# Both layers' MLP in blocks of 512 features, the first layer's with four seven-product pairs

## The chip, the cores and the metric

The kernel runs on one core of one Trainium2 chip. The metric is the device time of one execution in microseconds; the kernel before takes 2318.97 us, the median of three timed runs.

## What is computed

A trunk of two layers works on 640 tokens (128 context tokens, then 512 latent tokens) of width 1024. Each layer has a token mixer and a squared-ReLU MLP; the change touches the MLP.

```python
    sh1, sc1, g1, sh2, sc2, g2 = jnp.split(mod, 6, axis=-1)
    ...
    h = rmsnorm(x, lp['norm2_g']) * (1.0 + sc2) + sh2
    f = jnp.square(jax.nn.relu(h @ lp['w_mlp_in'])) @ lp['w_mlp_out']
    return x + g2 * f, k, v
```

`w_mlp_in` is 1024 by 4096, `w_mlp_out` is 4096 by 1024. `mod` comes from the conditioning vector of each group of tokens, so a residual add has one gain for columns 0 to 127 and another for columns 128 to 639.

## The kernel before, in words

**Layout.** Channels lie on the 128 partitions, the 640 tokens along the free dimension. Every float32 matrix is multiplied as two parts, h (rounded) and l (what is left): `split` (L239) makes h with an ACT copy (L240) and l with a DVE subtraction (L241), and a product takes three matmuls (h by h, h by l, l by h). A matmul covers 320 tokens, half of them, so a tile of 128 output channels with eight chunks of 128 inputs takes 8 x 3 x 2 = 48 matmuls, and one with four chunks 24.

**Weights.** They come as slabs of 128 by 1024 (512 KB). `ORDER` lists the slabs of each layer: `("i", j)` is the j-th 128 features of `w_mlp_in`, `("f", b, m)` is channel tile m of `w_mlp_out` for the 1024 features of block b, and `("h", b, i)` holds channel tiles 2i and 2i+1 for the 512 features of block b. `advance` has SP load them up to three ahead into four `raw` buffers and splits them up to two ahead into three pairs of buffers `wh`/`wl`. ACT and DVE work in an order that a scheduler fixes when the program is built; each engine then goes through its list in order. PE and SP follow the order of the code. Two priorities move instructions up in the scheduler's list: `SPLIT_FIRST` for weight splits and `EVAC_FIRST` for what empties PSUM.

**First layer's MLP before.** 32 input tiles (48 matmuls each) in four blocks of 8, each followed by ReLU on ACT (L1310), a square on DVE (L1311) and a split; after each block but the last, eight output tiles of 48 matmuls, each added to x by `residual` (L554) in three pieces (128, 192 and 320 columns). The last block goes through `project`, which also starts the next norm. PSUM has two buffers `ps`, one `sc`, one `pt`, one `po`. Beside this, `mod_dots` computes the second layer's modulation on DVE: 48 steps, each a load of 512 KB and two sums of products over 1024 columns (L490); `tick` moves it on by one step after each of these tiles.

**Second layer's MLP before** (`fast_mlp`). Six plain input tiles, then 13 pairs. A pair makes two input tiles from seven products of 12 matmuls (`prod`, L653) instead of 2 x 48 matmuls: 84 in place of 96. The products use sums of the activations' quarters (`t1` to `t4`, made once for each of four chunks on DVE, L627 to L638, and split into 16 tiles `t`) and sums of the weights (`one`, `two`, `three` in `Feed.pair`, L327 to L335). The first product of a pair is p1 (in `pt`, its right side the activations themselves), the second p5 (in `po`, its right side t1). `plus` (L659) adds the products up, L713 is ReLU and square in one. Between the products stand output tiles of blocks of 512 features (24 matmuls each); four per pair, until the last four pairs have 4, 2, 2 and 0.

## Time and profile before

| | us |
|---|---|
| median of 3 timed runs (2317.82 to 2321.76) | 2318.97 |
| the profiled execution, its own time | 2326.15 |
| its span, first to last instruction | 2324.4 |
| PE busy | 2254.2 (97%) |
| DVE busy | 1655.0 (71%) |
| ACT busy | 856.4 (37%) |

The first layer's MLP lies between about 734 and 1190 us of the span, the second layer's between about 1875 and 2324 us. Busy shares are averages over stages; what a change in one stage is worth shows in that stage, by the matmuls that PE starts in it and by what its gaps wait for.

### The profile page before, as it was taken

What the parts mean: (1) busy time and instruction counts of PE and PEld (TensorE: products, weight loads), DVE (VectorE), ACT (ScalarE), POOL (GpSimd) and SP (SyncE); (2) the same over time, 40 slices, a digit from 0 to 9 for tenths busy, and PEclk for the clock granted to TensorE, in tenths of its full rate; (3) what the DMA queues carried; (4) which work ended last, traced back from release to release, by engine and by line L of the source; (5) the groups of instructions that cost most, each with busy time, mean ns of one, the idle gap of its engine ahead of it and who ended that gap; (6) DMA issues with size and microseconds to landing.
All of it is one profiled execution on the core that took longest, in us unless ns stands there. A gap on an engine that the chain in (4) does not pass through costs nothing.

```text
span 2324.4 us, 36290 instructions
## 1 busy us (share of the span) xinstructions
PE 2254.2 (97%) x15050; PEld 2182.7 (94%) x15050; DVE 1655.0 (71%) x2557; ACT 856.4 (37%) x1296; POOL 70.4 (3%) x188
## 2 busy tenths in 40 slices
PE   6999999999999999999999999999999999999997
PEld 5989899989999999999998898999999999999987
DVE  6676457678777776766477773687897788777776
ACT  5455342222335332222254553422224453232233
POOL 1100000000000000000011000000000000000001
PEclk9999999999999999999999999999999999999999
DMA  7421122333343444444354212222222432222223
GB/s 285 113 84 60 63 70 99 133 136 136 126 138 127 154 154 146 151 148 146 108 175 107 78 46 69 73 78 64 65 76 92 150 109 65 73 85 89 73 91 110
DMA packets 77253, 252.43 MB, mean 109 GB/s; under 512 B 11808, under 2 KB 12832, under 8 KB 76960
## 3 DMA queue, kind: packets, MB, share of 16 engines
q1 hardware_dynamic: 66592, 224.56, 29.9%
q0 software_dynamic: 9920, 24.89, 3.8%
q8 instruction: 118, 1.93, 0.3%
q10 hardware_dynamic: 576, 0.66, 0.1%
q14 instruction: 47, 0.39, 0.1%
HBM read 238.65 MB, written 10.75 MB: 107 GB/s over the span
## 4 chain that ended last, share of the span: by engine, by line
PE 66%; issue 24%; DVE 6%; ACT 2%; DMA 1%; POOL 0%; SPq 0%; DVEq 0%; ACTq 0%; POOLq 0%
PE ps L362 44%; PE ph L362 5%; PE pt L653 4%; DVE l L241 2%; PE sc L653 2%; PE pt L857 1%; PE sc L846 1%; PE po L865 1%; PE sc L362 1%; ACT h L240 1%; PE po L653 1%; PE sc L1031 1%; DMA st<-in_w_mod 1%; PE pt L447 1%; PE sc L414 1%
## 5 line engine op out<-in xcount | busy, mean ns | idle before, releaser
L362 PE MATMUL ps<-h,h 128*128 128x320 f32 x5296 | 1119.3, 310 | 12.8 <-ACT gx L1132 4.7
L362 PEld LDWEIGHTS ps<-h,h 128*128 128x128 f32 x5296 | 862.7, 188 | 31.9 <-ACT h L240 12.5
L362 PE MATMUL ps<-h,l 128*128 128x320 f32 x3408 | 835.7, 309 | 0.0
L240 ACT ACTIVATE h<-raw 128x1024 fp32r<-128x1024 f32 x337 | 357.2, 1060 | 976.7 <-PE ps L362 658.8
L362 PEld LDWEIGHTS ps<-h,l 128*128 128x128 f32 x3408 | 585.6, 188 | 0.0
L241 DVE TENSOR_TENSOR l<-raw,h 128x1024 fp32r<-128x1024 f32 x337 | 411.6, 1222 | 217.5 <-ACT h L240 217.1
L362 PE MATMUL ps<-l,h 128*128 128x320 f32 x1520 | 384.6, 308 | 0.0
L362 PEld LDWEIGHTS ps<-l,h 128*128 128x128 f32 x1520 | 263.9, 188 | 0.3
L973 DVE SCALAR_TENSOR_TENSOR cv<-cv,cw,cv 128x655 f32<-128x655 f32 x240 | 215.9, 899 | 6.1
L554 DVE SCALAR_TENSOR_TENSOR x<-ps,mod,x 128x128 f32<-128x128 f32 (+2 forms) x260 | 99.8, 434 | 117.9 <-PE ps L362 117.8
L362 PE MATMUL ph<-h,h 128*128 128x320 f32 x768 | 179.6, 318 | 0.0
L362 PEld LDWEIGHTS ph<-h,h 128*128 128x128 f32 x768 | 129.1, 188 | 7.2
L240 ACT ACTIVATE h<-tmp 128x640 fp32r<-128x640 f32 (+1 forms) x92 | 67.5, 737 | 138.7 <-DVE tmp L1311 79.9
L362 PE MATMUL ph<-h,l 128*128 128x320 f32 x384 | 118.5, 309 | 0.0
L362 PE MATMUL ps<-bo,h 128*128 128x320 f32 x512 | 96.5, 309 | 1.8 <-DVE mg L1144 1.8
L241 DVE TENSOR_TENSOR l<-pt,h 128x512 fp32r<-128x512 f32 x84 | 57.9, 689 | 41.5 <-ACT h L240 41.3
L362 PEld LDWEIGHTS ps<-bo,h 128*128 128x128 f32 x512 | 80.2, 188 | 5.1 <-DVE mg L1144 2.4
L241 DVE TENSOR_TENSOR l<-tmp,h 128x640 fp32r<-128x640 f32 x92 | 74.9, 816 | 8.3 <-ACT h L240 8.3
L240 ACT ACTIVATE h<-pt 128x512 fp32r<-128x512 f32 x84 | 50.3, 599 | 77.1 <-PE pt L857 70.8
L490 DVE SCALAR_TENSOR_TENSOR junk<-raw,sw 128x1024 f32<-128x1024 f32 x48 | 58.8, 1224 | 25.4 <-DMA raw<-in_w_modt 25.2
L653 PE MATMUL pt<-h,h 128*128 128x320 f32 x260 | 71.4, 309 | 2.6 <-DVE tmp L659 2.6
L362 PEld LDWEIGHTS ph<-h,l 128*128 128x128 f32 x384 | 72.1, 188 | 0.0
(300 smaller groups left out, 2573.9 us busy)
## 6 DMA issues: line engine op xcount, KB each, us to landing
raw<-in_slabs SPq DMA_DIRECT2D x324, 512.0 KB, 3.6
raw<-in_w_modt SPq DMA_DIRECT2D x48, 512.0 KB, 3.7
md<-in_w_mod SPq DMA_DIRECT2D x32, 512.0 KB, 4.4
q<-qd POOLq DMA_DIRECT2D x18, 256.0 KB, 3.1
st<-in_w_mod SPq DMA_DIRECT2D x8, 512.0 KB, 9.7
raw<-in_w_mod SPq DMA_DIRECT2D x8, 512.0 KB, 7.1
x<-in_x SPq DMA_DIRECT2D x8, 320.0 KB, 6.0
qd<-h POOLq DMA_DIRECT2D x8, 320.0 KB, 9.1
```

What stands on the lines that cost most here:

```text
L240: act.activation(h, src, AF.Copy)
L241: (eng or vec).tensor_tensor(lo, src, _f(h), ALU.subtract)
L362: pe.matmul(v[:, c0:c1] if half is None else v, w_[:, kk, :], x_[:, c0:c1], start=first and pi == 0, stop=last and pi == 2)
L414: pe.matmul(v[:, c0:c1], ones, src[:, c0:c1], start=True, stop=True)
L447: pe.matmul(t[32 * q:32 * q + 32], sv3[:, 2 * kp + i, :], rr[i][j], start=kp == 0, stop=kp == 3)
L490: vec.scalar_tensor_tensor(out, w, 0.5, s3[s], ALU.mult, ALU.mult, accum_out=dst[:, c, s:s + 1])
L554: vec.scalar_tensor_tensor(xc[:, c0:c1], v[:, c0 - b0:c1 - b0], gv[:, c, s:s + 1], xc[:, c0:c1], ALU.mult, ALU.add)
L653: pe.matmul(v, w_[:, k0 + k, :], x_, start=k == 0 and pi == 0, stop=k == 3 and pi == 2)
L846: pe.matmul(v[:, c0:c1], lq, kk[:, SEQ + c0:SEQ + c1], start=pi == 0, stop=pi == 1)
L857: pe.transpose(pt[:, qt * P:(qt + 1) * P], parts[hd, qt][:, j * P:(j + 1) * P], ident)
L865: pe.matmul(po, vt[:, 1 + j, hd // 4, :], halves[hd, j][pi], start=j == 0 and pi == 0, stop=j == 4 and pi == 1)
L973: vec.scalar_tensor_tensor(y, b[:, j:j + CO], cw[:, c * CONV_K + j:c * CONV_K + j + 1], y, ALU.mult, ALU.add)
```

## The change

- The first layer gets the second layer's form: blocks of 512 features. Its first 24 input tiles are plain (48 matmuls each); from the fifth on, each is followed by the two output tiles of one `"h"` slab (24 matmuls each) for the block before. The last 8 input tiles are four seven-product pairs with 4, 2, 2 and 0 output tiles. The last 1024 features go through `project` as before. The second layer keeps six plain tiles and 13 pairs.
- `mod_dots` now moves on by two or three steps per plain input tile, and ends before the pairs; its buffers are given back, and the pairs' buffers are opened in their place. The quarter sums (`sums`) stand behind that point in the first layer, and beside the fifth tile, as before, in the second. The first layer, which doesn't keep the normed activations whole, adds h and l up again.
- The first layer's squares go from DVE to ACT for plain tiles. Residual adds of plain output tiles take two pieces (128 and 512 columns) in both layers.
- The first layer's slabs are loaded up to the layer's end by `Feed`; `advance` starts again at the second layer's first slab.

```diff
-FAST = (1,)
+PLAIN = (24, 6)
...
-    if l in FAST:
-        r += [("i", j) for j in range(5)] + [("h", 0, 0), ("i", 5), ("h", 0, 1)]
-        for b, p, fs in PAIRS:
-            r += [("i", 4 * b + 2 * p + i) for i in range(2)] + [("h", *f) for f in fs]
-        return r + 2 * [("f", 3, m) for m in range(8)]
-    r += [("i", j) for j in range(8)]
-    for b in range(4):
-        if b < 3:
-            r += [("i", 8 * (b + 1) + j) for j in range(8)]
-        r += [("f", b, m) for m in range(8)] * (2 if b == 3 else 1)
-    return r
+    r += [("i", j) for j in range(4)]
+    for j in range(4, PLAIN[l]):
+        r += [("i", j), ("h", j // 4 - 1, j % 4)]
+    for b, p, fs in PAIRS[l]:
+        r += [("i", 4 * b + 2 * p + i) for i in range(2)] + [("h", *f) for f in fs]
+    return r + 2 * [("f", 3, m) for m in range(8)]
...
+        def out_plain(w, m, fb):
+            v = _run(mtile(w, fb, k0=4 * (m % 2)))
+            for c0, c1, s in SEGS:
+                with later(-EVAC_FIRST):
+                    vec.scalar_tensor_tensor(x[m][:, c0:c1], v[:, c0:c1], mod3(l, 5)[:, m, s:s + 1], x[m][:, c0:c1], ALU.mult, ALU.add)
+
+        def sums():
...
+            for k in range(4):
+                s = tmp(T)
+                t1, t2 = s[:, a0:a1], s[:, b0:b1]
+                (h1, l1), (h2, l2) = ((_f(z) for z in h[k + n]) for n in (0, 4))
+                if keep:
+                    y1, y2 = keep[k], keep[k + 4]
+                else:
+                    y1, y2 = tmp(TH), tmp(TH)
+                    for y, (hh, lo) in ((y1, (h1, l1)), (y2, (h2, l2))):
+                        vec.tensor_tensor(y, hh[:, b0:b1], lo[:, b0:b1], ALU.add)
+                vec.tensor_tensor(t1, y1, h1[:, a0:a1], ALU.subtract)
+                vec.tensor_tensor(t1, t1, l1[:, a0:a1], ALU.subtract)
+                vec.tensor_tensor(t2, y2, t1, ALU.subtract)
+                if not keep:
+                    vec.tensor_tensor(y2, y2, y1, ALU.subtract)
+                    tb.append((k, y2))
+                    rest(k, s, y2, tslot, tb)
+                ta.append(split(s, tslot, T))
...
+        def rest(k, s, t3, tslot, tb):
+            h2, l2 = (_f(z)[:, a0:a1] for z in h[k + 4])
+            u = tmp(T)
+            vec.tensor_tensor(u[:, b0:b1], h2, l2, ALU.add)
+            vec.tensor_tensor(u[:, b0:b1], u[:, b0:b1], s[:, b0:b1], ALU.subtract)
+            vec.tensor_copy(u[:, a0:a1], t3)
+            tb[-1] = split(u, tslot, T)
...
+        for j in range(4, PLAIN[l]):
+            b, i = divmod(j, 4)
+            v = relu2(_run(mtile(use("i", j), h)))
+            fs_.setdefault(b, []).append(v)
+            tick()
+            if keep and j == 4:
+                quarters = sums()
+            w = use("h", b - 1, i)
+            for m in (2 * i, 2 * i + 1):
+                out_plain(w, m, fs_[b - 1])
+                if m % 2 or j % 2:
+                    tick()
+        if not keep:
+            flush()
+            dots.close()
+            open_room()
+        fd = Feed(room[0], (l + 1) * NS)
...
+        feed.append(fd)
+        fd.pump()
+        ta, tb = quarters or sums()
...
-                vec.tensor_tensor(r, r, r, ALU.mult)
+                if l + 1 < DEPTH:
+                    act.activation(r, r, AF.Square)
+                else:
+                    vec.tensor_tensor(r, r, r, ALU.mult)
...
+            if l + 1 < DEPTH:
+                nxt["dma"] = nxt["split"] = (l + 1) * NS
+                nxt["cap"] = ENDS[l + 1]
```

How the built programs' orders differ is shown at three places; in the rows a number behind a name tells one buffer's use from another's.

**PE, first layer's MLP, behind its 24th input tile, before.** `ps_9870` is the last output tile of the second block, `ps_9933` the 25th input tile (`h_6629` the activations, `h_9803` its weights).

```order
L362 MATMUL ps_9870<-h_8371,h_9740 128x320 x2
L362 MATMUL ps_9870<-l_8372,h_9740 128x320 x2
L362 MATMUL ps_9870<-h_8371,l_9741 128x320 x2
L362 MATMUL ps_9933<-h_6629,h_9803 128x320 x2
L362 MATMUL ps_9933<-h_6630,h_9803 128x320 x2
L362 MATMUL ps_9933<-h_6629,l_9804 128x320 x2
```

**PE at the same place, now.** `pt_10378` is the first pair's p1, which follows the last plain output tile `ps_10222` directly; `po_10393` is its p5 (`h_10311` and `l_10312` are the first chunk of t1, `h_10332` and `l_10333` the second, `h_10353` and `l_10354` the third, `h_10273` the weights).

```order
L702 MATMUL pt_10378<-h_6635,h_10269 128x320
L702 MATMUL pt_10378<-h_6636,h_10269 128x320
L702 MATMUL pt_10378<-h_6635,l_10270 128x320
L702 MATMUL po_10393<-h_10311,h_10273 128x320
L702 MATMUL po_10393<-l_10312,h_10273 128x320
L702 MATMUL po_10393<-h_10311,l_10274 128x320
L702 MATMUL po_10393<-h_10332,h_10273 128x320
L702 MATMUL po_10393<-l_10333,h_10273 128x320
L702 MATMUL po_10393<-h_10332,l_10274 128x320
L702 MATMUL po_10393<-h_10353,h_10273 128x320
L702 MATMUL po_10393<-l_10354,h_10273 128x320
```

The plain 25th tile has given way to a pair, whose second product reads what the quarter sums make; p1 is 12 matmuls, and p5 follows it at once.

**DVE at the same place, before.** The last output tile of the second block is added to x, with steps of `mod_dots` (`junk`, L490) and weight splits around it.

```order
L554 SCALAR_TENSOR_TENSOR x_6588<-ps_9870,mod_78,x_6588 128x128
L554 SCALAR_TENSOR_TENSOR x_6588<-ps_9870,mod_78,x_6588 128x192
L554 SCALAR_TENSOR_TENSOR x_6588<-ps_9870,mod_78,x_6588 128x320
L490 SCALAR_TENSOR_TENSOR junk_10125,mod_79<-raw_10056,sw_7571 128x1024
L241 TENSOR_TENSOR l_9930<-raw_9864,h_9929 128x1024
```

**DVE at the same place, now.** The last plain output tile `ps_10222` is added to x; around it stand the quarter sums (L630 to L633, L635, L655 to L657), of which those of the first chunk end with `l_10308` and `l_10312`.

```order
L615 SCALAR_TENSOR_TENSOR x_6588<-ps_10222,mod_78,x_6588 128x128
L615 SCALAR_TENSOR_TENSOR x_6588<-ps_10222,mod_78,x_6588 128x512
L657 COPY tmp_10303<-tmp_10296 128x320
L631 TENSOR_TENSOR tmp_10315<-tmp_10316,h_6631 128x320
L238 TENSOR_TENSOR l_10287<-raw_10257,h_10286 128x1024
L330 TENSOR_TENSOR raw_10277<-raw_10265,raw_10277 128x512
L655 TENSOR_TENSOR tmp_10324<-h_6639,h_6640 128x320
L632 TENSOR_TENSOR tmp_10315<-tmp_10315,h_6632 128x320
L238 TENSOR_TENSOR l_10308<-tmp_10303,h_10307 128x640
L238 TENSOR_TENSOR l_10312<-tmp_10294,h_10311 128x640
L633 TENSOR_TENSOR tmp_10315<-tmp_10317,tmp_10315 128x320
L630 TENSOR_TENSOR tmp_10337<-h_6633,h_6634 128x320
```

From the first of these rows to the last quarter sum's split there are 38 rows: 2 on `ps_10222`, 22 of 320 columns, 4 copies of 320, 8 splits of 640 (two for each chunk), one of 1024 and one of 512.

**DVE, the first layer's last pair, now**, the third place, in the step to `project`, whose first tile is `ps_11193`. Before, three output tiles of 48 matmuls stood here.

```order
L708 TENSOR_TENSOR tmp_11120<-pt_11123,tmp_11118 128x320
L751 SCALAR_TENSOR_TENSOR tmp_11163<-tmp_11120 128x640
L238 TENSOR_TENSOR l_11160<-raw_11023,h_11159 128x1024
L708 TENSOR_TENSOR tmp_11084<-sc_11137,tmp_11082 128x320
L238 TENSOR_TENSOR l_11166<-tmp_11163,h_11165 128x640
L751 SCALAR_TENSOR_TENSOR tmp_11169<-tmp_11084 128x640
L238 TENSOR_TENSOR l_11154<-raw_10927,h_11153 128x1024
L238 TENSOR_TENSOR l_11172<-tmp_11169,h_11171 128x640
L551 SCALAR_TENSOR_TENSOR x_6581<-ps_11193,mod_78,x_6581 128x128
```

These are the rows, in the same order, that end the second layer's pairs in both kernels.

## Rows read from the trace of the kernel before

**Rows 1.** The page's first part: busy us (share of the span), instructions.

```profile
PE 2254.2 (97%) x15050; PEld 2182.7 (94%) x15050; DVE 1655.0 (71%) x2557; ACT 856.4 (37%) x1296; POOL 70.4 (3%) x188
```

**Rows 2.** Windows, first layer's MLP: us, busy (count) by engine, PEclk, DMA.

```profile
737.00:1095.00 358.00, 358.00 (x2439) 357.66 (x2440) 255.40 (x394) 103.04 (x126) 0.00 (x0) 1.00 0.47 147
1095.00:1130.00 35.00, 35.00 (x241) 35.00 (x240) 11.33 (x20) 5.31 (x5) 0.00 (x0) 1.00 0.32 98
```

**Rows 3.** Windows, second layer's pairs, their last stretch and the first of `project`.

```profile
2150.00:2200.00 50.00, 50.00 (x343) 50.00 (x342) 38.25 (x66) 15.30 (x18) 0.00 (x0) 1.00 0.23 74
2200.00:2250.00 50.00, 47.39 (x320) 46.61 (x319) 36.36 (x60) 15.17 (x18) 0.00 (x0) 1.00 0.28 85
2250.00:2255.00 5.00, 2.61 (x16) 2.09 (x15) 4.55 (x6) 2.13 (x3) 0.00 (x0) 0.99 0.36 113
2255.00:2260.00 5.00, 5.00 (x26) 5.00 (x25) 0.00 (x0) 0.00 (x0) 0.00 (x0) 0.67 0.27 97
```

**Rows 4.** Waits, 2195 to 2262 us: engine, line, releaser: us in total, times, longest.

```profile
PEld pt L653 <- DVE tmp L659: 3.4, 3, 1.3
PE pt L653 <- DVE tmp L659: 2.6, 3, 1.1
PEld sc L362 <- DVE l L241: 2.1, 1, 2.1
PE sc L362 <- DVE l L241: 1.9, 1, 1.9
```

**Rows 5.** Timeline of DVE, second layer: start, us, line, tiles, count.

```profile
1909.94 1.69 DVE L627 TENSOR_TENSOR tmp<-f,h 128x320 f32<-128x320 f32 x4
1911.55 0.48 DVE L635 TENSOR_TENSOR tmp<-f 128x320 f32<-128x320 f32 x1
1911.95 0.48 DVE L636 TENSOR_TENSOR tmp<-h,h 128x320 f32<-128x320 f32 x1
...
1916.24 1.13 DVE L554 SCALAR_TENSOR_TENSOR x<-ps,mod,x 128x128 f32<-128x128 f32 x3
1917.28 1.28 DVE L629 TENSOR_TENSOR tmp<-f,tmp 128x320 f32<-128x320 f32 x3
...
1920.27 1.21 DVE L241 TENSOR_TENSOR l<-raw,h 128x1024 fp32r<-128x1024 f32 x1
1921.40 0.81 DVE L241 TENSOR_TENSOR l<-tmp,h 128x640 fp32r<-128x640 f32 x1
1922.14 0.48 DVE L637 TENSOR_TENSOR tmp<-tmp,h 128x320 f32<-128x320 f32 x1
...
1937.94 0.48 DVE L638 TENSOR_TENSOR tmp<-tmp,l 128x320 f32<-128x320 f32 x1
```

**Rows 6.** Groups by form, DVE and ACT: count, busy us, mean ns, idle before.

```profile
L738 DVE CAST place<-tmp 128x480 fp32r<-128x480 f32 x2 | 0.8, 410 | 1.5 <-DMA tmp<-in_place 1.5
L554 DVE SCALAR_TENSOR_TENSOR x<-ps,mod,x 128x320 f32<-128x320 f32 x88 | 47.8, 543 | 9.4 <-PE ps L362 9.4
L554 DVE SCALAR_TENSOR_TENSOR x<-ps,mod,x 128x128 f32<-128x128 f32 x86 | 30.1, 350 | 108.5 <-PE ps L362 108.4
L333 DVE TENSOR_TENSOR raw<-raw,raw 128x512 f32<-128x512 f32 x13 | 9.0, 689 | 0.3
L240 ACT ACTIVATE h<-tmp 128x640 fp32r<-128x640 f32 x90 | 66.2, 739 | 138.7 <-DVE tmp L1311 79.9 <-DVE tmp L1091 21.8 <-DVE tmp L713 21.4
L1310 ACT ACTIVATE tmp<-ps 128x640 f32<-128x640 f32 x36 | 24.7, 686 | 0.0
```

**Rows 7.** Line L490 (`mod_dots`): durations min/median/max, and what it waited for (us, times).

```profile
L490 DVE SCALAR_TENSOR_TENSOR junk<-raw,sw x48: 1217/1226/1228, 762.9 to 1090.3; 128x1024 f32<-128x1024 f32 x48
...
  DMA raw<-in_w_modt: 25.2, 35
```

**Rows 8.** DMA issues: size, median us from issue to landing.

```profile
raw<-in_slabs SPq DMA_DIRECT2D x324, 512.0 KB, 3.6
```

**Rows 9.** Windows, where the second layer's mixer begins.

```profile
1255.00:1260.00 5.00, 4.31 (x11) 2.51 (x10) 0.74 (x1) 2.09 (x3) 0.00 (x0) 0.50 0.80 114
1260.00:1265.00 5.00, 5.00 (x31) 5.00 (x30) 4.34 (x7) 2.96 (x5) 0.00 (x0) 0.84 0.54 179
```

More of the change, by code (lines that the diff above doesn't have):

```diff
@@ L55, with _pairs @@
 BR_ORDER = (0, 3, 2, 1)
-FAST = (1,)
-def _pairs():
-    due = [(b, mp) for b in range(6) for mp in range(4)]
+PLAIN = (24, 6)
+def _pairs(plain):
+    due = [(b, mp) for b in range(6) for mp in range(4)][plain - 4:]
     take = {(6, 1): 1, (7, 0): 1, (7, 1): 0}
     r = []
-    del due[:2]
-    for b in range(1, 8):
-        for p in range(1 if b == 1 else 0, 2):
-            n = take.get((b, p), 2)
-            r.append((b, p, due[:n]))
-            del due[:n]
+    for i in range(plain // 2, 16):
+        b, p = divmod(i, 2)
+        n = take.get((b, p), 2)
+        r.append((b, p, due[:n]))
+        del due[:n]
     assert not due
     return r
-PAIRS = _pairs()
+PAIRS = [_pairs(n) for n in PLAIN]
 def _order(l):
@@ L273, in trunk, with __init__ @@
     class Feed:
-        def __init__(self, mp):
+        def __init__(self, mp, end):
+            self.end = end
             self.w2 = maker(mp, "wh2", 1, 1024), maker(mp, "wl2", 1, 1024)
@@ L280, in __init__ @@
             self.todo, self.n, self.done = [], 0, set()
-            self.base = nxt["use"]
-            self.slab = self.base
+            self.slab = nxt["cap"] + 1
             self.got = {}
         def load(self, upto):
-            while self.slab < min(upto, len(order)):
+            while self.slab < min(upto, self.end):
                 l, s = order[self.slab]
@@ L608, in fast_mlp @@
             todo.append(fd.pair(i, [i + 2 + n for n in range(len(fs))]))
             i += 2 + len(fs)
-        fd.tail = {n: fd.plain(n) for n in range(i, len(order))}
-        f = [relu2(v) for v in vs]
-        f.append(relu2(_run(mtile(use("i", 3), h))))
-        f1 = [relu2(_run(mtile(use("i", 4), h)))]
-        def plain_tile(w, m, fb):
-            v = _run(mtile(w, fb, k0=4 * (m % 2)))
-            for half in range(2):
-                residual(x[m], v[:, HALVES[half][0]:], mod3(l, 5), m, half)
@@ L621, in fast_mlp @@
[L621 to L639 removed]
+        fd.tail = {n: fd.plain(n) for n in range(i, fd.end)}
@@ L684, in out_tile @@
                 fb, m, n, k = due.pop(0)
-                plain_tile(tuple(z.rearrange("p (k c) -> p k c", c=P) for z in ready[n]), m, fs_[fb])
+                out_plain(tuple(z.rearrange("p (k c) -> p k c", c=P) for z in ready[n]), m, fs_[fb])
                 if m % 2:
@@ L1303, in trunk @@
         with opened(f"ml{l}") as mp:
-            fast = l in FAST
-            fslot = maker(mp, "f", 16 if fast else 32, T)
+            fslot = maker(mp, "f", 16, T)
+            es = ExitStack()
             def relu2(v):
@@ L1310, in relu2 @@
                     act.activation(r, v, AF.Relu)
-                vec.tensor_tensor(r, r, r, ALU.mult)
+                if l + 1 < DEPTH:
+                    act.activation(r, r, AF.Square)
+                else:
+                    vec.tensor_tensor(r, r, r, ALU.mult)
                 return split(r, fslot, T)
-            def mlp_in(b):
-                out = []
-                if b == 0:
-                    out += [relu2(v) for v in first([("i", j) for j in range(3)], h, ss1, ab)]
-                for j in range(len(out), 8):
-                    out.append(relu2(_run(mtile(use("i", 8 * b + j), h))))
-                    tick()
-                return out
-            if l + 1 < DEPTH:
-                side.append(mod_dots(l + 1, mp))
-            f = fast_mlp(l, mp, h, ss1, ab, fslot, relu2) if fast else mlp_in(0)
-            for b in range(0 if fast else 3):
-                fn = mlp_in(b + 1)
-                for m in range(KC):
-                    v = _run(mtile(use("f", b, m), f))
-                    for half in range(2):
-                        residual(x[m], v[:, HALVES[half][0]:], mod3(l, 5), m, half)
-                    tick()
-                f = fn
-            flush()
+            f = paired_mlp(l, h, ss1, ab, fslot, relu2, es)
             if l + 1 < DEPTH:
```

73 lines of the change are left out of this document (34 added, 39 removed).

## The prediction

> **What bounds the kernel now.** Read the busy shares first: PE is busy 97% of the span, DVE 71%, ACT 37% [rows 1]. That average doesn't say whether a change in one stage counts, so the windows of the stage come next. In the first layer's MLP PE is busy without a gap: 35.00 of 35 us in the last stretch before `project`, and 358.00 of 358 before it [rows 2]. In a stretch without gaps PE starts 343 matmuls in 50 us (first row of [rows 3]), 0.1458 us each. So here the count of matmuls is the time, as long as DVE and ACT keep up, and DVE's 255.4 of 358 us [rows 2] say that there is room on the average. The second layer shows what the same form costs where it already stands: full speed in its middle, and gaps in its last stretch [rows 3]. The waits name who makes them: DVE [rows 4].
>
> **What it removes.** Four pairs at 84 instead of 96 matmuls: 48 fewer, 48 x 0.1458 = **-7.0 us**. All of them lie on the path, since PE has no gap there.
>
> **Squares, residuals, blocks.** Per plain step of the new order (one input tile, two output tiles) PE has 96 matmuls, 14.0 us. DVE's rows overlap a little: a row of 320 columns lasts 0.48 us and the next starts 0.40 us after it; for 640 columns it is 0.81 and 0.74, for 1024 columns 1.21 and 1.13; three pieces of a residual take 1.04 us [rows 5]. Two pieces: 0.350 for 128 columns, and for 512, on the line through 128 and 320 columns (0.350 and 0.543), 0.74 [rows 6], less two overlaps of 0.08: 0.92. A step then has two weight splits (2.26), one split of activations (0.74), two residuals (1.84) and on average 2.5 steps of `mod_dots` with two rows of 1.15 (5.75: 1.226 [rows 7] less the overlap, twice): 10.6 us of 14.0. ACT takes the square at about what it takes for a ReLU of 640 columns, 0.69 [rows 6]; it is far from full. This earns nothing, because PE already runs at full speed there, and it costs nothing as long as the 3.4 us of slack hold; I take 0, with -0 and +2 us as ends.
>
> **The way into the pairs.** In the second layer the quarter sums stand among plain tiles, from 1909.94 to 1938 us, and DVE is working without a break in the rows shown [rows 5]. In the first layer they now stand behind `mod_dots`, and the built order puts most of them behind the row that adds the last plain output tile, `ps_10222`, to x. DVE goes through its list in order and can't pass that row before PE has ended that tile. PE's next work is p1, 12 matmuls (1.75 us), and then p5, which needs the first chunk's split at once and the fourth's for its last three matmuls. From that row to the last split DVE has 38 rows: 22 x 0.40 = 8.8; 8 splits of 640 columns x 0.74 = 5.9; one of 1024, 1.13; one of 512, 0.61 (0.689 [rows 6] less 0.08); the residual 0.92; four copies at 0.33, from the cast of 480 columns, the nearest row (0.410 [rows 6] less 0.08): 1.3. That is 18.7 us. Behind the last copy ACT's rounding, 0.74 [rows 6], stands before DVE's last two splits and is not covered: 0.7; two matmuls remain, 0.3. So p5 ends 19.7 us after the last plain tile, where unhindered work would take 24 matmuls, 3.5 us: **+16.2 us**. Low end 15.2 (no hand-over), high end 19.2 (no overlap between rows: 21.7 in place of 18.7). Queued behind the waiting p5 are all of PE's rows; nothing else fills the hole, as PE follows the code. ACT's weight split for the third weight sum waits for the last plain tile too and takes about 1.1 us, less than DVE needs to get to it. The weights' own sums (`one`, `two`, `three`) are made earlier or in these rows, and their slabs land 3.6 us after issue [rows 8], while DVE has over 7 us of `mod_dots` between the release of their buffers and their first use: 0.
>
> **The clock behind the hole.** After PE's gap before `project` in the second layer the granted clock is 0.67 in the next 5 us, part of them at 1.2 instead of 2.4 GHz (last row of [rows 3]): 0.33 x 5 = **+1.7 us**. I take this row, as there, too, PE goes straight on to dense matmuls. By its count of 26 instead of 34.3 matmuls it is 1.2, the low end; the high end is 3.3, from 0.50 and 0.84 in the two 5-us stretches behind the hand-overs at the second mixer's start [rows 9].
>
> **The way out of the pairs.** The last four pairs have 4, 2, 2 and 0 output tiles, and rows in DVE's list in the same order as at the end of the second layer. There, from 2200 to 2260 us, PE starts 320 + 16 + 26 = 362 matmuls where 60 us hold 411.6 [rows 3]: 49.6 x 0.1458 = 7.2 us, the clock included; before the change the first layer had none of this (last row of [rows 2]). So **+7.2 us**. Ends: 4.5 (only the two waits of PE on DVE, 2.6 and 1.9 [rows 4]) and 8.2 (1 us more, if the loads of the second layer come in beside).
>
> **The next layer's start.** `advance` now begins anew at the second layer's first slab. The loads stand in SP's list directly behind the last `project` slabs and need 3.6 us [rows 8]; each half tile of `project` takes 24 matmuls, 3.5 us, and more than one is left by then: 0, between -1 and +1. Without that cover it would be a landing, ACT's and DVE's part of a split, some 6 us.
>
> **Sum.** -7.0 + 16.2 + 1.7 + 7.2 = +18.1 us. Made against the profiled execution's own 2326.15 us this gives 2344.3; the timed runs' median, 2318.97, lies 7.2 us (0.3%) below that execution, and the sum is taken over unchanged: **2337.1 us**, 0.8% slower.
>
> **A rule beside the trace.** The rows here overlap, as said: 0.48 us long, 0.40 us from start to start [rows 5]. The Trainium skill (VectorE: DVE Perf Modes, section The DRAIN you can't avoid) says that the next operation does not start until the pipe has emptied, though it adds that one that isn't held starts earlier. The trace bears out the second half of it.
>
> **Rivals.**
> - *No overlap.* If in the dependent chain of the sums each row waits for the one before to end, the 38 rows take 21.7 us, and the time is 2340.1. This is what the first half of the Trainium skill's rule (same page and section) comes to here. Against it: L635 and L636 write one tile's halves 0.40 us apart, and L637 starts 0.74 us after a split of 0.81 [rows 5]. Chance 0.05.
> - *`mod_dots` in fewer tiles.* Its 48 steps must now fit beside 20 plain steps. It waited for its loads 25.2 us in 35 places [rows 7], 0.72 each; 2.5 waits of this size make 12.4 of 14.0 us. At over 1.36 us each DVE falls behind, output tiles stay in PSUM and PE waits. At 1.7 us each, 10.6 + 4.3 = 14.9, and 20 steps lose 0.9 each: 18 us more, 2355. For it: two steps now often follow each other directly. Against it: the slack. Chance 0.08.
> - *DVE has a lead at the entry.* If the sums are ready when PE gets to p5, the hole and its clock go: 2337.1 - 17.9 = 2319.2, no change. It would need the 38 rows to be through by 1.75 us after the plain tiles; the built order speaks against it, the second layer's entry (PE without loss there) for it. Chance 0.07.
> - *The lead lasts to the end, faster than before.* It is the same mechanism, at `project`: with DVE ahead by the length of one pair's evacuation the 7.2 us go as well, and only the saved matmuls count: 2312.0. It decides at the last pair: the split of its tiles must be ready when `project`'s first three tiles have used the other chunks. Against it: the second layer, with nothing else on DVE, doesn't manage it [rows 3, 4]. Chance 0.05.
>
> **How the numbers follow.** The forecast has 0.75. Its ends: -7.0 + 15.2 + 1.2 + 4.5 - 1 = +12.9, 2332; -7.0 + 19.2 + 3.3 + 8.2 + 1 + 2 = +26.7, 2346. The first rival lies inside, so 2332 to 2346 holds 0.80, and what is left out is 0.08 above and 0.12 below. About 0.2% (4.6 us) is what a measurement can tell from no change. Slower by more: 0.75 + 0.05 + 0.08 = 0.88; within: 0.07; faster: 0.05.
>
> **What would show it.** Right: PE's p5 waits for DVE's split of a tmp tile four times in one pair and about 16 us in all, some 308 us after the MLP's start (2112 matmuls); a granted clock below 1 just behind; 343 matmuls per 50 us in the plain stretch; about 5 us of waits on DVE and a clock below 1 where `project` begins; 48 fewer matmuls in all. Wrong: the wait at p5 is a few us only (then the order left room, and 2319 is near), or x's adds in the plain stretch come late and PE waits for them there. What I am least sure of is the last term, since it is taken over from another layer.

## The result and the profile after

The changed kernel takes 2339.97 us (median of 4 timed runs, 2337.83 to 2343.24) beside 2318.85 us for the kernel before: a ratio of 1.009, 95% interval 1.0073 to 1.0108: slower by 0.9%. The forecast was 2337.1 us, with 2332 to 2346 as its range.

The profiled execution has a span of 2339.4 us, 15.0 us more than before. First the page, with busy time, share and count of each engine:

```profile
span 2339.4 us, 36281 instructions
PE 2246.2 (96%) x15002; PEld 2173.5 (93%) x15002; DVE 1700.3 (73%) x2605; ACT 881.7 (38%) x1332; POOL 70.1 (3%) x188
```

PE has 48 matmuls fewer than in [rows 1] and is busy 8 us less, but the span is longer. The stages tell where. Windows of the first layer's MLP (us; then busy time and count of PE, weight loads, DVE, ACT, POOL; granted clock, DMA share, GB/s):

```profile
737.00:1036.00 299.00, 293.70 (x1982) 291.93 (x1981) 226.35 (x357) 97.91 (x122) 0.00 (x0) 0.99 0.49 157
1036.00:1052.00 16.00, 15.67 (x107) 15.44 (x106) 15.52 (x30) 5.95 (x8) 0.00 (x0) 1.00 0.39 132
1052.00:1073.00 21.00, 8.03 (x29) 5.44 (x28) 18.65 (x40) 7.51 (x11) 0.00 (x0) 0.66 0.08 25
1073.00:1078.00 5.00, 5.00 (x28) 5.00 (x27) 1.08 (x3) 0.00 (x0) 0.00 (x0) 0.73 0.02 3
1078.00:1083.00 5.00, 5.00 (x36) 5.00 (x35) 2.53 (x4) 1.06 (x1) 0.00 (x0) 1.00 0.00 0
1083.00:1133.00 50.00, 49.06 (x335) 48.78 (x333) 37.40 (x58) 15.41 (x18) 0.00 (x0) 1.00 0.25 74
1143.00:1148.00 5.00, 4.04 (x28) 3.78 (x27) 3.20 (x6) 1.06 (x1) 0.00 (x0) 1.00 0.29 86
1153.00:1158.00 5.00, 3.13 (x21) 3.04 (x21) 2.65 (x4) 0.74 (x1) 0.00 (x0) 1.00 0.67 210
1158.00:1163.00 5.00, 5.00 (x37) 5.00 (x36) 1.59 (x3) 1.62 (x3) 0.00 (x0) 1.00 0.00 1
```

Read the count against the length. The plain stretch (737 to 1036 us) starts 1982 matmuls where the kernel before started 2037 in the same 299 us. Between 1052 and 1078 us 29 + 28 = 57 matmuls start, and 26 us have room for 178. And the last pairs and the start of `project`, from about 1130 to 1158 us, lose a little in each row shown.

For all kernels below a loss is worked out in one way: the time from the first matmul start of a stretch to that of the next, less 0.1458 us for each matmul. The stretches are the plain steps (1920 matmuls behind the fourth input tile; 1536 in the two kernels with six pairs), the first pair with its output tiles (180), the other pairs, and the first 48 matmuls of `project`. "Before" has no pairs in this layer; its third number is the 576 matmuls that stood in their place.

| kernel | median, us | ratio to before (95%) | plain | first pair | other pairs | `project`'s first 48 |
|---|---|---|---|---|---|---|
| before | 2318.85 | 1 | 1.8 | – | 0.5 | 1.5 |
| after | 2339.97 | 1.0090 (1.0073 to 1.0108) | 10.8 | 18.4 | 3.6 | 3.0 |
| sums early | 2336.30 | 1.0069 (1.0055 to 1.0083) | 21.0 | 0.2 | 3.6 | 4.5 |
| own buffers | 2339.77 | 1.0092 (1.0077 to 1.0107) | 12.0 | 18.2 | 3.6 | 3.0 |
| no loads | 2332.29 | 1.0052 (1.0039 to 1.0064) | 1.6 | 18.2 | 3.6 | 3.0 |
| even tail | 2347.56 | 1.0121 (1.0105 to 1.0136) | 12.0 | 19.7 | 3.9 | 4.5 |
| squares on DVE | 2347.23 | 1.0117 (1.0102 to 1.0132) | 13.8 | 19.2 | 3.6 | 4.2 |
| three pieces | 2342.75 | 1.0100 (1.0085 to 1.0115) | 9.0 | 18.9 | 3.7 | 3.0 |
| deep prefetch | 2339.81 | 1.0085 (1.0070 to 1.0100) | 6.7 | 19.3 | 3.6 | 4.5 |
| deep, sums at tile 21 | 2322.22 | 1.0007 (0.9997 to 1.0016) | 9.4 | 0.2 | 3.6 | 4.5 |
| other queue | 2332.75 | 1.0049 (1.0032 to 1.0066) | 2.3 | 17.8 | 3.6 | 3.0 |
| other queue, sums at tile 17 | 2320.05 | 1.0002 (0.9990 to 1.0013) | 6.1 | 0.2 | 3.6 | 3.0 |
| six pairs | 2317.47 | 0.9989 (0.9977 to 1.0000) | 6.0 | 0.2 | 3.8 | 0.7 |
| sums spread | 2313.37 | 0.9960 (0.9946 to 0.9973) | 2.2 | 0.2 | 3.9 | 0.7 |

The kernel before was run anew beside each group (2319 to 2322 us), so the ratios are what to compare. From its first matmul to the second layer's first, the MLP takes 480.2 us after and 455.4 us before: +24.9 us, which is -7.0 for the matmuls, +9.0 in the plain stretch, +18.4 at the first pair and +4.6 (3.6 + 3.0 less 0.5 + 1.5) on the way out.

**The way in.** Waits of PE between 1050 and 1080 us (engine, tile and line, releaser: us in total, times, longest), and the two ends of DVE's list there, with one place between them (start, duration, line, tiles; in brackets idle time and releaser):

```profile
PE po L702 <- ACT h L237: 7.9, 4, 3.1
PE po L702 <- DVE l L238: 5.0, 4, 2.6
```

```profile
1052.23 1.01 DVE L615 SCALAR_TENSOR_TENSOR x<-ps,mod,x 128x128 f32<-128x128 f32 x2 [0.16 <-PE ps L359]
...
1060.45 0.48 DVE L655 TENSOR_TENSOR tmp<-h,h 128x320 f32<-128x320 f32 x1
1060.85 0.49 DVE L632 TENSOR_TENSOR tmp<-tmp,h 128x320 f32<-128x320 f32 x1
...
1069.98 1.56 DVE L238 TENSOR_TENSOR l<-tmp,h 128x640 fp32r<-128x640 f32 x2 [0.80 <-ACT h L237]
```

p5 (in `po`) waits four times for the two parts of a split, once for each chunk. The two rows add up to 12.9 us. DVE goes from the last plain tile's residual at 1052.23 to the last split's end at 1071.54 us: 19.3 us, with one gap of 0.80 us at ACT's rounding, so that the 38 rows themselves take 18.5. By the starts of PE's matmuls, 16.6 of the 18.4 us lie between p1's last matmul and p5's last, and 1.7 in the 14 intervals behind it, which are 0.27 us long instead of 0.147. The clock is low from 1058.6 us, within the hole, to 1075.7 (0.66 and 0.73 in the two windows above).

**The plain stretch.** Waits between 735 and 1052 us, then DVE's timeline at one place, then SP's rows for the load that DVE waits for there:

```profile
DVE junk L487 <- DMA raw<-in_w_modt: 56.1, 38, 3.3
PE ps L359 <- DVE x L615: 5.5, 7, 2.1
```

```profile
767.58 1.22 DVE L487 SCALAR_TENSOR_TENSOR raw<-raw,sw 128x1024 f32<-128x1024 f32 x1
...
773.01 1.22 DVE L487 SCALAR_TENSOR_TENSOR junk<-raw,sw 128x1024 f32<-128x1024 f32 x1 [2.40 <-DMA raw<-in_w_modt]
774.16 0.08 DVE L487 DVE_READ_ACCUMULATOR junk<-raw,sw 128x1 f32 x1
774.16 0.82 DVE L238 TENSOR_TENSOR l<-tmp,h 128x640 fp32r<-128x640 f32 x1
774.90 1.00 DVE L615 SCALAR_TENSOR_TENSOR x<-ps,mod,x 128x128 f32<-128x128 f32 x2
```

```profile
768.84 0.33 SPq L477 DMA_DIRECT2D raw<-in_w_modt  x1
770.64 0.33 SPq L248 DMA_DIRECT2D raw<-in_slabs  x1
```

The waits for `mod_dots`' loads have gone from 25.2 us in 35 places [rows 7] to 56.1 in 38. At 773 us DVE has stood still for 2.40 us for a block, and the residual of an output tile that PE had finished at about 772 us stands behind it in DVE's list, at 774.90. PE then wants the buffer `ps` back and waits, 5.5 us in 7 places, each at the first matmul of the input tile of a step, in every second step; behind the longest of them the clock is low for 3.4 us (952.8 to 956.2 us). The block was asked for only at 768.84, as DVE's row on the block before ended. SP's own waits say the same of the whole stretch (735 to 1052 us): its loads of blocks (L477) wait 140.6 us for the buffers that DVE's rows on a block (L487) give back.

```profile
SPq L477 <- DVE raw L487: 140.6, 34, 6.1
```

### The profile page after: what moved, and what is told of

The parts are those of the page before. It is cut to its first block, busy times and chain, and to the rows that moved or that the text cites. A ratio compares the mean times of both kernels' runs of the same rounds, so it can differ in the third digit from the quotient of the medians.

```text
span 2339.4 us, 36281 instructions
## 1 busy us (share of the span) xinstructions
PE 2246.2 (96%) x15002; PEld 2173.5 (93%) x15002; DVE 1700.3 (73%) x2605; ACT 881.7 (38%) x1332; POOL 70.1 (3%) x188
## 4 chain that ended last, share of the span: by engine, by line
PE 77%; DVE 12%; DMA 6%; issue 3%; ACT 3%; SPq 0%; DVEq 0%; POOL 0%; ACTq 0%
PE ps L359 53%; PE ph L359 5%; PE pt L702 5%; DMA raw<-in_w_modt 5%; DVE l L238 3%; PE sc L702 2%; PE sc L359 2%; DVE junk L487 2%; PE pt L895 1%; PE sc L884 1%; PE po L702 1%; ACT h L237 1%; PE po L903 1%; PE sc L1069 1%; DMA st<-in_w_mod 1%
## 5 line engine op out<-in xcount | busy, mean ns | idle before, releaser
L359 PE MATMUL ps<-h,h 128*128 128x320 f32 x5040 | 1071.9, 311 | 16.8 <-DVE x L615 5.5
L359 PEld LDWEIGHTS ps<-h,h 128*128 128x128 f32 x5040 | 822.2, 188 | 37.0 <-ACT h L237 10.3
L359 PE MATMUL ps<-h,l 128*128 128x320 f32 x3280 | 807.2, 309 | 0.0
L359 PEld LDWEIGHTS ps<-h,l 128*128 128x128 f32 x3280 | 564.6, 188 | 0.0
L238 DVE TENSOR_TENSOR l<-raw,h 128x1024 fp32r<-128x1024 f32 x341 | 416.5, 1221 | 187.4 <-ACT h L237 187.1
L615 DVE SCALAR_TENSOR_TENSOR x<-ps,mod,x 128x128 f32<-128x128 f32 x192 | 96.6, 545 | 39.5 <-PE ps L359 39.5
L237 ACT ACTIVATE h<-tmp 128x640 fp32r<-128x640 f32 (+1 forms) x100 | 72.8, 735 | 83.3 <-DVE tmp L751 27.3
L487 DVE SCALAR_TENSOR_TENSOR junk<-raw,sw 128x1024 f32<-128x1024 f32 x48 | 58.8, 1224 | 56.3 <-DMA raw<-in_w_modt 56.1
L702 PE MATMUL pt<-h,h 128*128 128x320 f32 x340 | 93.6, 310 | 5.0 <-DVE tmp L708 5.0
L238 DVE TENSOR_TENSOR l<-tmp,h 128x640 fp32r<-128x640 f32 x100 | 81.4, 817 | 12.1 <-ACT h L237 12.0
L702 PE MATMUL pt<-h,l 128*128 128x320 f32 x272 | 83.8, 308 | 0.0
```

The lines of the kernel that those rows point to most:

```text
L237: act.activation(h, src, AF.Copy)
L238: (eng or vec).tensor_tensor(lo, src, _f(h), ALU.subtract)
L359: pe.matmul(v[:, c0:c1] if half is None else v, w_[:, kk, :], x_[:, c0:c1], start=first and pi == 0, stop=last and pi == 2)
L487: vec.scalar_tensor_tensor(out, w, 0.5, s3[s], ALU.mult, ALU.mult, accum_out=dst[:, c, s:s + 1])
L615: vec.scalar_tensor_tensor(x[m][:, c0:c1], v[:, c0:c1], mod3(l, 5)[:, m, s:s + 1], x[m][:, c0:c1], ALU.mult, ALU.add)
L702: pe.matmul(v, w_[:, k0 + k, :], x_, start=k == 0 and pi == 0, stop=k == 3 and pi == 2)
```

## Experiments

Four questions: what makes the hole at the first pair, what makes the plain stretch slow, what the last pairs cost, and what the two small edits are worth. All edits are made to the changed kernel; where one is made on top of another run's, the text says so, and its diff shows what is new. Lines move by a few between kernels, and the scheduler orders ACT's and DVE's rows anew for each.

### The hole at the first pair: the sums made early

```diff
+        tpool = es.enter_context(opened(f"tq{l}"))
...
-            tslot = maker(room[0], "t", 16, T)
+            tslot = maker(tpool, "t", 16, T)
...
-            if keep and j == 4:
+            if j == (4 if keep else 12):
```

> The first layer's quarter sums are made beside its 13th input tile, in buffers of their own, and no longer behind the last plain tile. Theory (the hole at the first pair is DVE's 38 rows of sums queued behind the last plain residual): the first pair runs without a gap, the clock stays at 1.00 behind it, and the 17.9 us of hole and clock go; but 18.7 us of DVE work now stand beside plain steps that have at most 3.4 us of slack each, so that PE may lose up to 10 us more there. Time 2322 to 2332. Rival (p5 waits for something else that DVE does there, such as the pair's weight sums, or DVE is late from the plain stretch): the first pair still waits 10 us or more, 2335 to 2341.

Measured 2336.30 us, a time in the rival's range, but the trace speaks for the theory: the first pair loses 0.2 us instead of 18.4, so the hole was DVE's sums. But the plain stretch now loses 21.0 us instead of 10.8. Waits of PE in the first layer's MLP, and ACT's timeline in the steps where the sums now stand:

```profile
PE ps L359 <- DVE x L616: 13.1, 11, 3.9
```

```profile
905.66 1.37 ACT L237 ACTIVATE h<-tmp 128x640 fp32r<-128x640 f32 x2 [8.40 <-DVE tmp L658]
...
916.24 1.37 ACT L237 ACTIVATE h<-tmp 128x640 fp32r<-128x640 f32 x2 [6.70 <-DVE tmp L658]
919.32 0.70 ACT L1349 ACTIVATE tmp<-ps 128x640 f32<-128x640 f32 x1 [1.72 <-DVE l L238]
```

DVE is behind, and so is ACT: it waits up to 8.40 us for a sum that it is to round, and a ReLU that would free `ps` stands behind that in ACT's list (L1349 at 919.32). Of the 18.2 us that the first pair gains, 10.2 have moved to the plain stretch.

### The plain stretch: four ways to bring the blocks

Own buffers: two for `mod_dots` alone, loads still one block ahead.

```diff
-            t = raw_tile()
+            t = mp.tile([P, 1024], F32, tag="wm", bufs=2, name=nm("wm"))
```

> The loads of mod_dots get two buffers of their own and no longer share the four raw buffers with the weight slabs. Theory (in the plain stretch DVE waits for a mod_dots load that is issued only when its buffer comes free, and output tiles wait behind it): the DVE waits for these loads go from 56 us to under 15 us, PE's gaps at every second plain step and the half clock behind the last of them go: 8.9 us less, 2331 (2329 to 2334). Rival (three mod_dots steps in every second plain step are simply too much work for DVE): the gaps stay, 2338 to 2341. Second rival (the 512 KB loads are late because they share the DMA engines with the slabs): the waits stay above 35 us, and 2336 to 2341.

No loads:

```diff
-            t = raw_tile()
-            sp.dma_start(out=t, in_=a["w_modt"][v, c])
-            return t
+            if not held:
+                held.append(mp.tile([P, 1024], F32, tag="wm", bufs=1, name=nm("wm")))
+                sp.dma_start(out=held[0], in_=a["w_modt"][v, c])
+            return held[0]
...
-                out = w if s else junk()
+                out = junk()
```

> mod_dots loads its first block only and uses it 48 times: the other 47 loads are left out, so the second layer's modulation is that of another matrix; DVE's rows are all there. Theory (waits for loads) and the rival that the loads share the DMA engines: no waits, 2331 (2329 to 2333), as with buffers of their own or better. Rival (too many DVE rows in every second step): 2338 to 2341.

Own buffers change nothing in time (2339.77 us, plain stretch 12.0; DVE's waits for blocks go from 56.1 only to 41.4 us), so that the shared `raw` buffers alone were the cause falls. Without the loads the plain stretch loses 1.6 us and the kernel takes 2332.29, as the theory had it, with all 96 of DVE's rows on blocks still there (they end earlier, at 964 instead of 1036 us): too much work for DVE falls as well. It is the loads' arrival. Two explanations were left: too short a lead, or something that holds the loads back. Deep prefetch tries the first:

```diff
-            t = raw_tile()
+            t = mp.tile([P, 1024], F32, tag="wm", bufs=4, name=nm("wm"))
...
-        w = fetch(*blocks[0])
+        ws = [fetch(*b) for b in blocks[:3]]
...
-            wn = fetch(*blocks[i + 1]) if i + 1 < len(blocks) else None
+            w = ws.pop(0)
+            if i + 3 < len(blocks):
+                ws.append(fetch(*blocks[i + 3]))
...
-            w = wn
```

> mod_dots gets four buffers of its own and issues each load three blocks ahead (two own buffers with the load one block ahead left the plain stretch's loss at 11.9 us; leaving the loads out took it to 1.6). Theory: with one block of lead a load can be issued only when DVE is done with the block before, takes about 4 us to land, and DVE needs 2.3 us for a block, so where two or three blocks stand in a row DVE waits, and the residual queued behind the waiting row keeps PE's buffer; three blocks of lead cover that: waits for these loads under 5 us in all, the plain stretch loses under 3 us, 2330 (2328 to 2334). Rival: loads come late because the slabs take the DMA engines' time; then the lead doesn't help, waits stay above 25 us, 2337 to 2341.

2339.81 us: the rival's time, and waits of 30 us remain, longer ones in fewer places. The lead isn't without effect: the plain stretch loses 6.7 us instead of 10.8, and the first pair (0.9) and `project`'s start (1.5, the clock) take 2.4 of these 4.1 back. Its waits, then its DVE and SP rows, show why three blocks of lead don't help more:

```profile
DVE junk L489 <- DMA wm<-in_w_modt: 30.0, 14, 3.9
```

```profile
SPq L248 <- DVE l L238: 211.0, 35, 19.1
SPq L477 <- DVE wm L489: 10.8, 4, 4.0
```

```profile
863.67 1.22 DVE L238 TENSOR_TENSOR l<-raw,h 128x1024 fp32r<-128x1024 f32 x1
...
877.17 1.21 DVE L238 TENSOR_TENSOR l<-raw,h 128x1024 fp32r<-128x1024 f32 x1
...
883.39 1.23 DVE L489 SCALAR_TENSOR_TENSOR junk<-wm,sw 128x1024 f32<-128x1024 f32 x1 [3.44 <-DMA wm<-in_w_modt]
```

```profile
864.91 0.33 SPq L248 DMA_DIRECT2D raw<-in_slabs  x1
865.29 0.43 SPq L477 DMA_DIRECT2D wm<-in_w_modt  x1
...
878.41 0.33 SPq L248 DMA_DIRECT2D raw<-in_slabs  x1
878.78 0.91 SPq L477 DMA_DIRECT2D wm<-in_w_modt  x2
```

Each slab goes out as DVE's split gives a `raw` buffer back (863.67 + 1.22 = 864.89; 877.17 + 1.21 = 878.38), and each block's load goes out 0.37 to 0.38 us behind a slab's. SP works through its list in order: a block whose own buffer is free stands behind a slab whose buffer isn't. SP's waits bear it out: 211.0 us for the buffers of slabs (L248), 10.8 for those of blocks (L477). The rival's reason, the shared DMA engines, is tried by the next run, the deep prefetch with GpSimd issuing the same loads:

```diff
-            sp.dma_start(out=t, in_=a["w_modt"][v, c])
+            pool.dma_start(out=t, in_=a["w_modt"][v, c])
```

> As with the deep prefetch (four own buffers, three blocks ahead), and the loads of mod_dots are issued by GpSimd instead of SyncE. With SyncE the deep prefetch still waited 30 us for these loads in 14 places, and its plain stretch lost 6.6 us. Theory: on SyncE a mod_dots load stands in order behind a slab load that waits for its raw buffer; on its own queue it goes out as soon as its buffer is free, waits fall under 8 us, the plain stretch loses under 2.5 us, so 8 to 10 us less than the changed kernel: 2329 to 2333, with the hole at the first pair unchanged. Rival (the loads are late because all slabs and blocks share the DMA engines, or because a block takes about 4 us on any queue): waits stay above 20 us, plain stretch 5 us or more, 2335 to 2341.

2332.75 us, and no wait of DVE for a block is left in the trace. The window of the plain stretch:

```profile
737.00:1036.00 299.00, 299.00 (x2037) 298.45 (x2036) 230.80 (x373) 101.70 (x126) 23.37 (x44) 1.00 0.50 158
```

2037 matmuls, as many as the kernel before starts there. The DMA engines carry as much as before, and a block's load still takes 4.7 us from issue to landing (4.6 with SP, both medians between 800 and 930 us, where 34 blocks are loaded beside 22 with SP). So, with the lead there, it was the place in SP's list that still held the loads: the plain stretch loses 2.3 us instead of 6.7. The rest of the 7 us between the two runs lies mostly at the first pair and at `project`'s start, 1.5 us each. Another queue with one block of lead was not tried. The Trainium skill (DMA: Bandwidth & Descriptors, section Rules for kernel authors) says that spreading DMAs over SP, ACT and GpSimd doesn't help bandwidth, as they run on the same DMA engines, and only saves issue time. The landing times agree with it; what another queue gave here is that a load doesn't stand behind another load's wait.

The scheduler has also placed the blocks' rows closer, up to four to a step, so that they end at 934 us. Between 761 and 929 us DVE has no room at all, and PE loses nothing by it (1143 matmuls in 168 us):

```profile
761.00:929.00 168.00, 168.00 (x1143) 167.45 (x1143) 167.75 (x280) 52.29 (x64) 23.37 (x44) 1.00 0.68 213
```

DVE is busy 167.75 of 168 us here, and 226.35 of 299 in the changed kernel, which loses 9 us. So DVE's busy share doesn't tell here whether PE waits; whether a row that stands ahead of a residual has itself to wait does.

### The way out: output tiles for the last pair

```diff
-    take = {(6, 1): 1, (7, 0): 1, (7, 1): 0}
+    take = {(6, 0): 1, (6, 1): 1, (7, 0): 1, (7, 1): 1}
```

> The last four pairs of both layers get 2, 2, 2, 2 output tiles in place of 4, 2, 2, 0. Theory (where project begins, PE waits because the last pair has nothing between its products and project that covers ACT and DVE): the waits there shrink by about the length of one output tile and more, 2 to 5 us in each layer, and the clock drop at the second layer's end is rarer: 2331 to 2337. Rival (the cover only moves: the pair before loses what the last gains): 2338 to 2341.

2347.56 us, worse than either expected. The losses in the first layer: `project`'s first 48 matmuls 4.5 us, the first pair, which gives up two output tiles, 1.3 us more. In the second layer its pairs and its `project` lose 1.5 us more each. Waits of PE where the first layer's `project` begins, and the windows there:

```profile
PE sc L359 <- DVE l L238: 1.9, 1, 1.9
PE sc L359 <- ACT h L237: 0.5, 1, 0.5
```

```profile
1153.00:1158.00 5.00, 2.61 (x16) 2.09 (x16) 5.00 (x7) 2.42 (x3) 0.00 (x0) 1.00 0.37 105
1158.00:1163.00 5.00, 5.00 (x26) 5.00 (x25) 0.22 (x1) 0.00 (x0) 0.00 (x0) 0.66 0.28 108
```

The two waits at `project` are as long as in the changed kernel (1.9 and 0.5 us), so two output tiles gave no cover for that hand-over. The clock is 0.66 behind them, where the changed kernel's stayed at 1.00 (its window 1158 to 1163: 37 matmuls in place of 26). That is the 1.5 us between 3.0 and 4.5; it also stands in the rows "sums early" and "deep prefetch", in which nothing was changed here. What would shorten the hand-over wasn't found.

### The two small edits, undone

Squares back on DVE, and residuals in three pieces:

```diff
-                if l + 1 < DEPTH:
+                if False:
                     act.activation(r, r, AF.Square)
```

> The first layer's squares go back from ScalarE to DVE, all else as changed. By the prediction's step the squares on ScalarE earn nothing where PE is at full speed; but the plain stretch now loses 9 to 11 us because DVE is late, and 20 squares of 0.74 us are 14.8 us of DVE work more there. Theory (each plain step that is late is late by DVE's whole list): 0.4 to 0.74 us more in ten or more steps, 2344 to 2352. Rival (DVE waits for loads anyway, and the square fits into that wait): 2338 to 2342.

2347.23 us: 6.3 us more by the ratios (1.0117 less 1.0090, with intervals that just overlap), a time in the theory's range. In the trace the plain stretch loses 3.0 us more, and PE's waits for residuals there are 9.9 us in 9 places, where the changed kernel has 5.5 in 7. So the squares on ScalarE, put at 0, are worth some 3 us in this order; the rest of the 6.3 is not accounted for.

```diff
-            for c0, c1, s in SEGS:
-                with later(-EVAC_FIRST):
-                    vec.scalar_tensor_tensor(x[m][:, c0:c1], v[:, c0:c1], mod3(l, 5)[:, m, s:s + 1], x[m][:, c0:c1], ALU.mult, ALU.add)
+            for half in range(2):
+                residual(x[m], v[:, HALVES[half][0]:], mod3(l, 5), m, half)
```

> Residual adds of plain output tiles in three pieces again, in both layers, all else as changed: 1.04 instead of 0.92 us each, 40 of them in the first layer's plain stretch (4.8 us of DVE in all) and some in the pairs. Theory (late steps are late by DVE's list): 1 to 4 us more, 2341 to 2344. Rival (the piece is hidden): 2338 to 2341.

2342.75 us, in the theory's range, but the interval of its ratio overlaps that of the changed kernel, and its plain stretch loses less (9.0 us), not more. The ratios differ by 2.3 us, less than their intervals can tell from nothing, so what the two pieces are worth stays open.

### Both causes mended

On top of deep prefetch, three blocks in every plain step, and the sums behind the 21st input tile:

```diff
-                if m % 2 or j % 2:
-                    tick()
-        if not keep:
-            flush()
-            dots.close()
-            open_room()
+                tick()
+            if not keep and j == 20:
+                flush()
+                dots.close()
+                open_room()
+                quarters = sums()
```

> As with the deep prefetch, and mod_dots moves on by three blocks in every plain step, so that it ends at the 21st input tile; its buffers are given back there and the quarter sums are made beside the last three plain steps. Theory: DVE has 11.7 us of 14.0 in a three-block step and about 11 in a step with sums, so neither the plain stretch nor the first pair loses: 8.9 and 17.9 us go, leaving -7.0 from the matmuls and about +5 at the way out: 2313 to 2319, not slower than before the change. Rival (DVE's order, not its amount of work, makes PE wait: any of its rows that stand ahead of a residual): the plain stretch keeps 5 us or more, 2319 to 2328.

2322.22 us, the rival's range. The first pair is free, the plain stretch loses 9.4 us. Windows of three stretches in a row:

```profile
980.00:995.00 15.00, 15.00 (x104) 15.00 (x104) 6.12 (x9) 4.19 (x5) 0.00 (x0) 1.00 0.23 72
995.00:1015.00 20.00, 20.00 (x138) 20.00 (x137) 14.91 (x32) 6.81 (x9) 0.00 (x0) 1.00 0.27 79
1015.00:1025.00 10.00, 7.80 (x42) 7.30 (x40) 9.38 (x20) 3.31 (x5) 0.00 (x0) 0.83 0.16 52
```

DVE is busy 6.12 of 15 us, then 9.38 of 10, and there PE starts 42 matmuls instead of 69, 3.9 of the 9.4 us. It has the time, only earlier. So the next run gives the blocks to GpSimd's queue, six of them ahead of the fifth tile, and puts the sums behind the 17th input tile:

```diff
+        if not keep:
+            for _ in range(6):
+                tick()
...
-            if not keep and j == 20:
+            if not keep and j == 16:
```

> As with the other queue, and mod_dots moves on by six blocks ahead of the fifth tile and three in each plain step, ends at the 17th input tile, and the quarter sums stand behind that tile, eight input tiles before the first pair; 24 plain tiles as in the change. With sums at the 21st tile DVE was idle ahead of them and then late in the last steps (5 us lost there). Theory: here neither the plain stretch nor the first pair loses: 2312 to 2317, between no difference from the kernel before and 0.3% faster. Rival (sums beside plain steps always cost PE some 5 us, as DVE's list puts them ahead of residuals): 2317 to 2324.

2320.05 us, the rival's range. The first pair and every plain step but one run at full speed; one step, behind the sums, loses 3.6 us. With 20 plain tiles, six pairs and the sums behind the 16th tile:

```diff
-PLAIN = (24, 6)
+PLAIN = (20, 6)
...
-            if not keep and j == 16:
+            if not keep and j == 15:
```

> As the run before, but with 20 plain tiles and six pairs in the first layer (24 more matmuls fewer, 3.5 us) and the sums behind the 16th input tile, four tiles before the first pair. Theory: the pairs run as the second layer's pairs do, without loss until the last ones, so 3.5 us less than with 24 plain tiles: 2308 to 2314, faster than the kernel before by 0.2 to 0.5%. Rival (mod_dots, sums and weight sums stand too close together, DVE is late at the first pairs): 2314 to 2324.

2317.47 us, the rival's range again, and no difference from the kernel before. The pairs do run as the theory had it (0.2 and 3.8 us), but the same step loses 3.9 us, and ACT's timeline shows it once more: 5.47 us of waiting for a sum, with a slab's part and a ReLU behind it.

```profile
944.08 1.37 ACT L237 ACTIVATE h<-tmp 128x640 fp32r<-128x640 f32 x2 [5.47 <-DVE tmp L658]
945.45 1.06 ACT L237 ACTIVATE h<-raw 128x1024 fp32r<-128x1024 f32 x1
946.41 0.69 ACT L1352 ACTIVATE tmp<-ps 128x640 f32<-128x640 f32 x1
```

The last run makes the sums one chunk at a time, behind the 16th to the 19th tile:

```diff
                 ta.append(split(s, tslot, T))
+                yield ta, tb
...
-            return ta, tb
+            yield ta, tb
...
-                quarters = sums()
+                parts = sums()
+            if not keep and 15 <= j < 19:
+                quarters = next(parts)
...
```

> As the run with six pairs, but the quarter sums are made one chunk at a time behind the 16th to 19th input tiles. All at once behind the 16th they cost PE 3.9 us in one step (a ReLU stands behind the sums' roundings in ScalarE's list, and a residual behind the sums in DVE's). Theory: 4.7 us of sums in each of four steps fit beside the 4.8 us that DVE has there without mod_dots; the plain stretch loses 2 to 2.5 us instead of 6.0, and the time falls by 3 to 4 us: 2312 to 2315 beside 2319 to 2322 for the kernel before, faster by 0.2 to 0.4%. Rival (the sums cost the same wherever they stand, a little in each step): 2316 to 2319, no difference from the kernel before.

2313.37 us beside 2322.14 for the kernel before it was run with: 0.996 (0.9946 to 0.9973), the theory's range, and faster than the kernel before and the changed one. The windows of the same 60 us, first with the sums at once and then spread:

```profile
907.00:967.00 60.00, 56.66 (x385) 56.13 (x384) 51.70 (x93) 23.72 (x30) 0.23 (x1) 1.00 0.28 85
```

```profile
907.00:967.00 60.00, 60.00 (x411) 59.95 (x410) 50.33 (x88) 22.07 (x29) 0.53 (x1) 1.00 0.31 94
```

## Why the prediction was right, and where it was not

- **-7.0 us, fewer matmuls:** right, 48 fewer.
- **Squares, residuals, blocks, 0 (up to +2):** the step that failed; +9.0. It set 10.6 us of DVE work, on the average of a step, against 14.0, and took the slack as cover. The work was sized rightly: DVE is busy 212 of 275 us between 761 and 1036, 10.8 us of 14.0. But the waits were not priced at their new size (56.1 us in 38 places, 1.5 each, where the step counted none and the rival 0.72), and the average hid the place. Spread over 20 steps they are 2.8 us each, and 10.6 + 2.8 = 13.4 of 14.0 would still say 0. A block's row stands ahead of a residual, so that a late load goes straight to PE, though DVE idles elsewhere. The rival "`mod_dots` in fewer tiles" comes nearest, as it has the waits; but it lets PE wait only when they fill a step, and was given 0.08, and 18 us against the 9.0 measured. That it is the loads, and not DVE's amount of work, "no loads" shows, and so does "other queue", where DVE is full and PE doesn't wait. As far as the runs tell, what made them late was the lead of one block, and, with that mended, their place in SP's list.
- **The way in, +16.2, and the clock behind it, +1.7:** together 17.9, measured 18.4, of which 16.6 in p5 and 1.7 behind it. The 38 rows with their hand-over were put at 18.7 + 0.7 us; DVE took 19.3. "Sums early", in which the first pair loses 0.2 us, shows that nothing else of this size holds p5. The low end should have been 16.2 less 0.7, 15.5 and not 15.2; it changes nothing here. The price of "no overlap" (21.7 us for the rows) falls at 18.5 measured: L655 and L632 start 0.40 us apart at 0.48 us each. Here, too, the trace speaks for the second half of the rule that the prediction cited from the Trainium skill (VectorE: DVE Perf Modes, section The DRAIN you can't avoid), that a next op which isn't held starts earlier.
- **The way out, +7.2 (4.5 to 8.2):** +4.6. The pairs' end and `project`'s start lost 6.6 us (3.6 + 3.0), near the 7.2. But the prediction took it that the kernel before lost nothing there, from a row that ends at 1130 us, ahead of `project` [rows 2]; it lost 2.0, of which 1.5 where `project` begins. The 7.2 had the second layer's fall of the clock in it [rows 3]; here the waits were there (`pt` for DVE, 2.5 us, then `sc` for the last split, 1.9), but the clock stayed at 1.00. In other runs it fell, for 1.5 us.
- **The next layer's start, 0:** no loss, as foretold: the terms above add up to the whole MLP's +24.9, and the second layer's first 80 matmuls take 1.4 us less than before.
- **The sum:** +18.1 foretold, +24.9 in the profiled MLP, +21.1 in the medians. Outside the MLP the two profiled executions differ by 9.9 us in favour of the changed one: 3.1 ahead of the MLP (its first matmul starts at 731.24 instead of 734.36 us), where before had a clock drop in the first mixer, and 6.8 behind it. Of these, 2.7 us at the second mixer's start come back in every kernel with 24 plain tiles (below), and 24.9 - 2.7 = 22.2 is near the medians' 21.1. The forecast lay 2.9 us low: one term too small by 9.0, one too large by 2.6, and a gain behind the MLP that it didn't have. That it lay so near is luck in part: the 9.0 us, against an upper end of 2, were mostly taken back by two things that it didn't foresee.
- **Its signs:** the four waits of p5, the low clock and the 48 matmuls were there. So was one of its signs of being wrong: x's adds came late in the plain stretch, and PE waited 5.5 us for them.

## What to carry to other kernels

An engine that is busy 11 of 14 us can still stop another one, and one that is busy 14 of 14 need not: ask for each row that may wait what stands behind it in the same list, give loads a lead, and put those whose buffers are free into a queue where nothing waits ahead of them. One-off work for a form that saves matmuls (here 19 us of sums for 7.0 us of matmuls, 10.5 with six pairs) has to be spread over stages that have the room, or it takes back what the form saves, in part or whole: 18.4 us in one block just ahead of its use, 3.6 to 3.9 in one step, and no pause of PE when spread over four.
